# Ordering the instructions of a two-layer RWKV-7 / Hyena / mixture-of-experts kernel with the simulator's timeline model

## Chip, cores and metric

The kernel runs on one core of one Trainium2 chip. The metric is the device time of one execution in microseconds (us), lower is better. TensorE is called PE here, its weight loads PEld, VectorE is DVE, ScalarE is ACT, GpSimd is POOL, and SyncE, which issues most DMAs, is SP.

## What is computed

Two layers over 512 latent and 256 context tokens of width 1024, in fp32. The reference, cut to what matters:

```python
for l in range(2):
    p = modulate(x, shift, scale) @ w_in[l]          # 43 blocks of 128 columns, context tokens too
    y_r = rwkv7(p_rwkv)                              # two scans over the tokens, forward and backward:
    #   S <- S diag(w) + (S (-kk)) (kk*a)^T + v k^T ; y = S r        8 heads x 64
    y_h = x0 * (irfft(rfft(v*x1) * rfft(filt)) + bias * (v*x1))      # long convolution, 512 channels
    g_r, g_h = split(sigmoid(p_gate))
    s = (g_r * (y_r @ w_branch[0]) + g_h * (y_h @ w_branch[1])) @ w_out
    x = layer_norm(alpha * x + gate * s)
    # mixture of experts: best of 4 groups by its two best scores, then two experts inside it
    x = layer_norm(alpha * x + gate2 * moe(modulate(x)))
```

In the second layer the context tokens are no longer carried past the start of the scans, so its row counts are smaller (512 tokens in the gates, where the first layer has 512 and 256).

## The kernel before

The body is Python that emits instructions in program order inside a `tile.TileContext`. The order in which an engine gets its instructions is not the order of the Python text: the context's scheduler takes the instructions that are ready, by the priority they were emitted with and by a table of durations for each kind of instruction, and writes out one fixed list for each engine. Each engine then works its list strictly from the top, and waits where an operand is not there. Two stretches are scheduled apart, because a loop whose number of rounds is only known on the chip (experts with more rows than their place; no round runs here) lies between them: everything up to that loop in the first layer, and all after it.

Each layer goes through these stages:

- **project** (L733 to L1088): the modulated input times `w_in`, each block of 128 columns split into a high and a low part (`hi`, `lo`, L588, L589) and multiplied in three passes (matmuls `pl` for latent and `px` for context tokens, L853 to L860), and the Hyena convolution by matrices of the discrete Fourier transform. For each channel group and segment the convolution is a chain: transposes `hz<-con,zf` (L1005), split in hi and lo, the forward transform (matmuls of `mm3`, L593 to L595, `dft...` tables), products on DVE and POOL (L1015 to L1020), transposes `hz<-con,Y` (L1026), split again, and the inverse transform (`idft...` tables). Blocks of the projection can stand between these links.
- **RWKV** (L1108 on, class `Rwkv`): per pair of token chunks a front part (small matmuls `psl` L248, `pE` L310, `pO` L311, with DVE, ACT and POOL work between), the inverse of a triangular matrix (chain of `pw` L417, `pz` L425, `pw` L435, `pz` L445 with DVE at both ends), then the chain over chunks (L494 to L532). There are three such pairs in each layer. Into this stage the second part of the gates is emitted last (L1126 to L1136): for each of 6 (first layer) or 10 (second layer) blocks of 128 gate columns eight matmuls `gp` (L1133) over 512 tokens, and in the first layer eight more over 256, one sigmoid (L1135) and a store. `gp` has one PSUM bank. `GATES = (10, 6)` (L38) is the number of gate blocks that are computed earlier.
- **branch and merge** (L1220 to L1360): `pb` (the two branches times `w_branch`, with L593 to L595), `po` (the product with `w_out`), the residual and LayerNorm on DVE (L1315 to L1342), the result `h` stored by SP to `hd` (L1344), transposed (`ph`, L1350) and taken through the router matmul (`plg`, L1354), then the routing on DVE (L1554 to L1600).
- **experts** (L1602 on): SP loads the expert weights in 1 MB pieces (`raw<-in_w_exp`, L2148), reads expert numbers into registers (L1887, and L1837 for the number of rounds), POOL gathers token rows (`xg<-hd,idx`, L1924), and PE multiplies (`acc`, L2000 and L2003).

```python
for j in range(GATES[l], 16):                        # L1126
    ...
    for a, n in segs:                                # 512 tokens, and 256 in the first layer
        p = gp.tile([128, 512], F32, name="gp", tag="gp")
        for k in range(8):
            nc.tensor.matmul(p[:, :n], raw[k // 4][:, k % 4], self.gx[...], start=k == 0, stop=k == 7)   # L1133
```

## Time and profile before

| what | us |
|---|---|
| three runs | 3240.1, 3251.25, 3238.47 (median 3240.1) |
| the profiled execution | 3255.05, of which the span is 3253.3 |
| busy in the span | PE 2942.1, DVE 1668.5, ACT 1127.5, POOL 573.6 |
| first layer | project 0 to 526, RWKV 526 to 892, branch and merge to 1117, experts to 1784 |
| second layer | project to 2151, RWKV to 2530, branch and merge to 2660, experts to 3254 |

The busy time of an engine is the time in which at least one of its instructions ran; the stages were cut by hand at the instructions that open them. The profiled execution is one run, and differs from the median of the others by 15 us. The fp32 matmuls without a split appear as two records each in the trace, so that `x6` of `L1133` stands for three matmuls.

### The profile page before, as it was taken

To read this page: it belongs to the slowest core of one execution; us is meant where nothing else is said; L and a number is where in the kernel's file an instruction comes from. 1 tells how busy PE (TensorE), PEld (TensorE's weight loads), DVE (VectorE), ACT (ScalarE), POOL (GpSimd) and SP (SyncE) were. 2 spreads that over 40 slices of the span, in tenths; PEclk is the share of its full clock that TensorE was granted. 3 is DMA by queue.
4 is the path that set the end of the run, shared out by engine and by line. 5 is a ranking of instruction groups with operands and counts; after the bars stand their busy time and mean duration, and the time that the engine had idled before them with its cause. 6 is when DMAs were issued, how large, how long until landed. Compare 5 with 4: busy or idle time off the path is not lost. (4 is left out here: it accounts for less than half of the span.)

```text
span 3253.3 us, 61441 instructions
## 1 busy us (share of the span) xinstructions
PE 2942.1 (90%) x25238; PEld 2018.5 (62%) x25238; DVE 1668.5 (51%) x2981; ACT 1127.5 (35%) x2293; POOL 573.6 (18%) x458
## 2 busy tenths in 40 slices
PE   7999999888888799999997999979889879999994
PEld 5877866676677566555663767646666655444551
DVE  4466534787766544435645347447876571111223
ACT  3453225566421233323422434255554221111111
POOL 1001221354004200000022001254340120000002
PEclk8999999899999799999998899987999979999997
DMA  5453274111244689998895464451112549999995
GB/s 225 126 154 99 80 254 137 51 50 52 84 149 166 242 337 367 358 351 328 322 359 216 153 198 121 156 174 57 50 50 87 205 168 360 383 402 421 383 373 235
DMA packets 220870, 689.83 MB, mean 212 GB/s; under 512 B 71813, under 2 KB 99750, under 8 KB 169128
## 3 DMA queue, kind: packets, MB, share of 16 engines
q1 hardware_dynamic: 186280, 588.62, 49.0%
q10 hardware_dynamic: 26448, 70.73, 6.1%
q0 software_dynamic: 7856, 26.49, 2.3%
q8 instruction: 202, 3.31, 0.4%
q14 instruction: 84, 0.69, 0.1%
HBM read 621.46 MB, written 64.30 MB: 211 GB/s over the span
## 5 line engine op out<-in xcount | busy, mean ns | idle before, releaser
L2000 PE MATMUL acc<-raw,x 128*64 128x256 f32 (+1 forms) x7168 | 569.8, 334 | 13.7 <-DMA raw<-in_w_exp 13.6
L2000 PEld LDWEIGHTS acc<-raw,x 128*64 128x64 f32 (+1 forms) x7168 | 358.3, 125 | 213.9 <-issue 90.9
L589 DVE TENSOR_TENSOR lo<-raw,hi 128x1024 fp32r<-128x1024 f32 x190 | 229.5, 1231 | 303.2 <-ACT hi L588 295.9
L2003 PE MATMUL acc<-raw,a 128*64 128x512 f32 (+2 forms) x1376 | 292.6, 602 | 7.3 <-DMA raw<-in_w_exp 6.2
L588 ACT CAST hi<-raw 128x1024 fp32r<-128x1024 f32 x190 | 193.5, 1048 | 294.6 <-PE px L857 149.9
L2031 DVE TENSOR_TENSOR act<-acc,act 128x256 f32<-128x256 f32 (+1 forms) x98 | 42.1, 430 | 442.5 <-PE acc L2000 400.2
L853 PE MATMUL pl<-xh,hi 128*128 128x512 f32 x560 | 228.1, 407 | 0.2
L858 PE MATMUL pl<-xh,lo 128*128 128x512 f32 x560 | 224.7, 401 | 0.3 <-DVE lo L589 0.3
L854 PE MATMUL pl<-xl,hi 128*128 128x512 f32 x560 | 224.1, 400 | 0.0
L2003 PEld LDWEIGHTS acc<-raw,a 128*64 128x64 f32 (+2 forms) x1376 | 79.0, 130 | 179.9 <-issue 160.5
L1133 PE MATMUL gp<-gx,raw 128*128 128x512 f32 (+1 forms) x352 | 174.2, 612 | 1.6 <-ACT gs L1135 1.5
L1924 POOL DMA_INDIRECT xg<-hd,idx x31 | 31.5, 1015 | 780.8 <-PE pt L1942 706.1
L853 PEld LDWEIGHTS pl<-xh,hi 128*128 128x128 f32 x560 | 107.0, 191 | 44.3 <-issue 20.3
L2026 ACT ACTIVATE act<-acc 128x256 f32<-128x256 f32 (+1 forms) x98 | 38.0, 387 | 241.3 <-PE acc L2000 206.0
L2051 ACT COPY a<-pt 128x256 f32<-128x256 f32 (+2 forms) x86 | 28.5, 349 | 261.6 <-PE pt L2046 261.6
L858 PEld LDWEIGHTS pl<-xh,lo 128*128 128x128 f32 x560 | 107.2, 191 | 18.3 <-issue 10.1
L2057 DVE TENSOR_TENSOR sum<-acc,sum 64x512 f32<-64x512 f32 x82 | 56.4, 687 | 117.6 <-ACT sum L2056 116.9
L854 PEld LDWEIGHTS pl<-xl,hi 128*128 128x128 f32 x560 | 107.1, 191 | 13.7 <-issue 6.2
L311 PE MATMUL pO<-T,K 128*128 128x192 f32 (+1 forms) x320 | 84.9, 378 | 29.0 <-DVE T L330 27.4
L856 PE MATMUL px<-xh,hi 128*128 128x256 f32 x376 | 110.2, 294 | 0.0
L2056 ACT COPY sum<-acc 64x512 f32<-64x512 f32 x82 | 47.6, 580 | 179.3 <-PE acc L2003 178.2
L857 PE MATMUL px<-xl,hi 128*128 128x256 f32 x376 | 108.5, 289 | 0.1
(607 smaller groups left out, 6178.0 us busy)
## 6 DMA issues: line engine op xcount, KB each, us to landing
raw<-in_w_exp SPq DMA_DIRECT2D x384, 1024.0 KB
mraw<-in_w_mod SPq DMA_DIRECT2D x64, 512.0 KB
raw<-in_w_in SPq DMA_DIRECT2D x36, 512.0 KB
rkk<-rkk SPq DMA_DIRECT2D x24, 768.0 KB
raw<-in_w_in ACTq DMA_DIRECT2D x34, 512.0 KB
mraw<-in_w_mod SPq DMA_DIRECT2D x12, 1024.0 KB
raw<-in_w_in SPq DMA_DIRECT2D x32, 256.0 KB
wb<-in_w_branch SPq DMA_DIRECT2D x32, 256.0 KB
```

Source lines behind the costliest of these rows:

```text
L311: nc.tensor.matmul(pO[:, jj, 0:192], lO, T[c][kO, j, 1, :], start=True, stop=True)
L588: self.nc.scalar.copy(hi, src)
L589: (engine or self.nc.vector).tensor_tensor(lo, src, f32(hi), ALU.subtract)
L853: mm(pl, hi[:, k], xh[:, k, L], start=f, stop=False)
L854: mm(pl, hi[:, k], xl[:, k, L], start=False, stop=False)
L856: mm(px, hi[:, k], xh[:, k, X], start=f, stop=False)
L857: mm(px, hi[:, k], xl[:, k, X], start=False, stop=False)
L858: mm(pl, lo[:, k], xh[:, k, L], start=False, stop=e)
L1133: nc.tensor.matmul(p[:, :n], raw[k // 4][:, k % 4], self.gx[:, k, a - T0:a - T0 + n], start=k == 0, stop=k == 7)
L2000: mm(a[w * g:w * g + w, 0:4 * w], x, raw[:, 4 * w * g:4 * w * g + 4 * w], start=k == 0, stop=k == 7)
L2003: mm(a[w * g:w * g + w], x, raw, start=k < G, stop=k >= 8 - G)
L2057: tt(t, a[o:o + 64], t, ALU.add)
```

## The change

The context is told to schedule with the simulator's timeline model: while it picks the next instruction for each engine it takes ready times and durations from that model, and no longer from its own table. Priorities, tiles, buffers, semaphores and the program itself stay as they are.

```diff
-    with tile.TileContext(nc) as tc:
+    with tile.TileContext(nc, schedule_with_timeline_sim=True) as tc:
         Kern(tc, A).run()
```

The number and kind of the instructions on each engine are the same, but for four fewer ACT_TABLE_LOADs on ACT, which follow from the order of its functions. What moves is the order; three places are shown.

**PE at the entry of RWKV in the second layer.** `hz` L710 is the modulation, `gp` the gates, `psl`, `pE` and `pO` the front part, `pw` L417 the first step of the first inverse. Before:

```order
L710 MATMUL hz<-mraw,c_78 32x512 x7
L1133 MATMUL gp<-gx,raw 128x512
L724 MATMUL pq<-mrow,con 2x512
L1133 MATMUL gp<-gx,raw 128x512
L248 MATMUL psl<-lw,w_16284 128x128 x4
L1133 MATMUL gp<-gx,raw 128x512 x2
L248 MATMUL psl<-la,a_16285 128x128 x4
L1133 MATMUL gp<-gx,raw 128x512 x2
L248 MATMUL psl<-lw,w_16284 128x128 x4
```

With the change:

```order
L1133 MATMUL gp<-gx,raw 128x512 x8
L710 MATMUL hz<-mraw,c_78 32x512 x6
L1133 MATMUL gp<-gx,raw 128x512 x8
L724 MATMUL pq<-mrow,con 2x512
L1133 MATMUL gp<-gx,raw 128x512 x8
L248 MATMUL psl<-lw,w_16284 128x128 x4
L1133 MATMUL gp<-gx,raw 128x512 x8
L248 MATMUL psl<-la,a_16285 128x128 x4
L1133 MATMUL gp<-gx,raw 128x512 x8
L248 MATMUL psl<-lw,w_16284 128x128 x4
```

Whole groups of eight now stand between the pieces of the front part. In the second layer 24 of the 80 `gp` matmuls stood ahead of the first `pw` of L417, now all 80. In the first layer 16 of 48 with 512 columns and 15 of 48 with 256 stood ahead of it, now 48 and 40.

**PE in the Hyena convolution of the first layer**, one link of its chain: the transposes `hz<-con,Y` and what follows them. `pl` and `px` are blocks of the projection. Before:

```order
L1026 MATMUL hz<-con,Y 128x128 x3
L858 MATMUL pl<-xh,lo 128x512
L1026 MATMUL hz<-con,Y 128x128 x3
L860 MATMUL px<-xh,lo 128x256
L853 MATMUL pl<-xh,hi 128x512
L854 MATMUL pl<-xl,hi 128x512
L856 MATMUL px<-xh,hi 128x256
L593 MATMUL hz<-idftlh,yh 128x256
```

With the change, the like link of the last channel group:

```order
L593 MATMUL hz<-dftlh,zh 128x384
L594 MATMUL hz<-dftll,zh 128x384
L595 MATMUL hz<-dftlh,zl 128x384
L1026 MATMUL hz<-con,Y 128x128 x6
L593 MATMUL hz<-idftlh,yh 128x256
L594 MATMUL hz<-idftll,yh 128x256
L595 MATMUL hz<-idftlh,yl 128x256
```

No block stands between the links there; in the last two channel groups of the first layer nine links follow one another like this, and runs of 16 and 21 rows of blocks stand between others.

**PE and SP in the merge of the second layer.** On PE before, where `po` is the output product of later tokens and `ph`, `plg` the transposes and router product of `h`:

```order
L593 MATMUL po<-oh,mh 128x512
L1350 MATMUL ph<-con,h__23749 128x128 x4
L594 MATMUL po<-ol,mh 128x512
L595 MATMUL po<-oh,ml 128x512
L593 MATMUL po<-oh,mh 128x512
L594 MATMUL po<-ol,mh 128x512
L1350 MATMUL ph<-con,h__23749 128x128 x4
L1354 MATMUL plg<-wrt,hT 128x16 x4
```

On PE with the change, from the last `po` on:

```order
L595 MATMUL po<-oh,ml 128x512
L1350 MATMUL ph<-con,h__23680 128x128 x8
L1354 MATMUL plg<-wrt,hT 128x16 x8
L1350 MATMUL ph<-con,h__23749 128x128 x8
L1354 MATMUL plg<-wrt,hT 128x16 x8
L1350 MATMUL ph<-con,h__23864 128x128 x8
```

On SP before, where `hd` is the store of `h`, `raw` a weight load, and L1887 reads an expert's number:

```order
L1344 DMA hd<-h__23680 128x1024
L1344 DMA hd<-h__23749 128x1024
L2148 DMA raw<-in_w_exp 128x2048
L1344 DMA hd<-h__23864 128x1024
L2148 DMA raw<-in_w_exp 128x2048 x2
L1344 DMA hd<-h__23933 128x1024
L2148 DMA raw<-in_w_exp 128x2048 x9
L1887 TENSOR_LOAD eid
```

On SP with the change:

```order
L1344 DMA hd<-h__23680 128x1024
L1344 DMA hd<-h__23749 128x1024
L2148 DMA raw<-in_w_exp 128x2048 x10
L1344 DMA hd<-h__23864 128x1024
L1344 DMA hd<-h__23933 128x1024
L1887 TENSOR_LOAD eid
```

All `po` now stand ahead of the first `ph`; ten weight loads, where there were three, stand ahead of the last `hd` store; and SP reads 12 expert numbers at once, where it read three and went on with weights.

## Rows read from the trace of the kernel before

**Rows 1.** The page: span, busy time of PE, and its clock in 40 slices.

```profile
span 3253.3 us, 61441 instructions
...
PE 2942.1 (90%) x25238; PEld 2018.5 (62%) x25238; DVE 1668.5 (51%) x2981; ACT 1127.5 (35%) x2293; POOL 573.6 (18%) x458
...
PEclk8999999899999799999998899987999979999997
```

**Rows 2.** Busy time in stretches; `(x...)` counts records; last clock, DMA share, GB/s.

```profile
core 0: us, PE busy (x) PEld busy (x) DVE busy (x) ACT busy (x) POOL busy (x), PEclk, DMA share, GB/s
...
100.00:526.00 426.00, 408.05 (x2243) 318.38 (x2241) 204.78 (x321) 145.25 (x229) 58.77 (x66) 0.98 0.47 148
526.00:601.50 75.50, 61.17 (x308) 41.18 (x304) 60.30 (x117) 51.69 (x142) 32.14 (x34) 0.86 0.26 85
601.50:864.00 262.50, 237.69 (x4207) 185.75 (x4207) 201.63 (x417) 144.09 (x409) 94.43 (x78) 0.93 0.18 57
...
2151.00:2217.00 66.00, 54.96 (x265) 33.70 (x264) 47.83 (x93) 47.76 (x136) 35.35 (x41) 0.84 0.33 107
...
2660.00:3254.00 594.00, 528.00 (x4555) 270.41 (x4554) 130.54 (x264) 85.07 (x184) 43.51 (x31) 0.95 0.90 358
```

**Rows 3.** Timeline of PE in RWKV of the first layer: start, duration, instruction.

```profile
534.03 2.84 PE L1133 MATMUL gp<-gx,raw 128*128 128x512 f32 x6
...
547.89 3.72 PE L1133 MATMUL gp<-gx,raw 128*128 128x256 f32 x16
...
554.51 1.98 PE L1133 MATMUL gp<-gx,raw 128*128 128x512 f32 x4 [0.54 <-ACT gs L1135]
```

**Rows 4.** Busy time of the gates alone (L1133), PE and PEld, by stretch.

```profile
601.50:864.00 262.50, 56.88 (x131) 23.39 (x130) 0.93 0.18 57
...
2217.00:2530.00 313.00, 62.42 (x112) 20.05 (x112) 0.90 0.21 65
```

**Rows 5.** Busy time inside RWKV: fronts, and inverses with gates in them.

```profile
680.00:710.00 30.00, 22.55 (x132) 16.74 (x132) 27.74 (x49) 16.86 (x52) 13.32 (x12) 0.77 0.18 58
710.00:741.00 31.00, 30.23 (x612) 22.78 (x612) 25.65 (x59) 16.75 (x42) 7.65 (x6) 1.00 0.14 40
790.00:816.00 26.00, 19.04 (x102) 12.50 (x103) 25.20 (x43) 11.60 (x34) 11.86 (x10) 0.80 0.05 16
...
2217.00:2252.00 35.00, 32.77 (x640) 22.89 (x640) 22.47 (x56) 15.40 (x39) 7.07 (x7) 0.81 0.13 40
```

**Rows 6.** Chain of waits, 2217 to 2327: pieces of the path.

```profile
2217.24 3.42 PE pw L417 x128
...
2227.15 3.38 PE gp L1133 x4
```

**Rows 7.** Chain of waits, 2327 to 2424: a piece of the path.

```profile
2327.35 2.04 PE pw L417 x126
```

**Rows 8.** Timeline of PE in the first layer's Hyena convolution.

```profile
359.37 0.60 PE L1005 MATMUL hz<-con,zf 128*128 128x128 f32 x4
...
361.93 0.44 PE L593 MATMUL hz<-dftlh,zh 128*128 128x384 f32 x1
...
366.62 0.33 PE L595 MATMUL hz<-dftlh,zl 128*128 128x384 f32 x1
...
368.75 0.55 PE L1026 MATMUL hz<-con,Y 128*128 128x128 f32 x3 [0.50 <-POOL Y L1019]
```

**Rows 9.** Busy time at the end of the first layer's chain.

```profile
864.00:892.00 28.00, 22.97 (x320) 18.20 (x319) 24.80 (x56) 19.60 (x42) 0.00 (x0) 0.94 0.22 73
```

**Rows 10.** Timeline of DVE in the second layer's merge.

```profile
2632.10 0.17 DVE L1355 COPY lgt<-plg 128x16 f32<-128x16 f32 x1 [4.16 <-PE plg L1354]
...
2642.12 0.17 DVE L1355 COPY lgt<-plg 128x16 f32<-128x16 f32 x1 [1.38 <-PE plg L1354]
...
2653.69 0.17 DVE L1355 COPY lgt<-plg 128x16 f32<-128x16 f32 x1 [5.36 <-PE plg L1354]
```

**Rows 11.** Timeline of all engines, from the second layer's merge to its experts.

```profile
2638.38 0.33 SPq L2148 DMA_DIRECT2D raw<-in_w_exp  x1
...
2664.59 1.22 POOL L1924 DMA_INDIRECT xg<-hd,idx  x1 [9.34 <-DVE x L1712]
...
2673.30 1.54 PE L1942 MATMUL pt<-con,xg 96*128 96x96 f32 x8 [9.78 <-DMA xg<-hd,idx]
```

**Rows 12.** What SP's queue waited for: total us, times, longest.

```profile
SPq L2148 <- PE acc L2000: 459.9, 183, 27.1
```

**Rows 13.** SP at L1887, the reading of expert numbers: ns min/median/max, first and last start.

```profile
L1887 SPq TENSOR_LOAD <-eid x30: 260/270/469, 1110.8 to 3122.1; - x30
L1887 SPq FUSED_REGOPS  x30: 147/152/181, 1111.3 to 3122.4; - x30
```

**Rows 14.** Groups of instructions: a table load on ACT, busy time and mean ns.

```profile
L1135 ACT ACT_TABLE_LOAD x13 | 16.7, 1283 | 0.2
```

## The prediction

> **What bounds the kernel now.** I read the page first. PE is busy in 2942.1 of 3253.3 us, 90%, and no other engine comes near it [rows 1]; so a new order can gain at most what PE is idle or runs at a low clock, and it can lose wherever it puts PE work where something was waiting behind PE. The clock row shows which stages run below full speed [rows 1]. Then I read the stretches one by one, because the 90% is a mean over stages with different limits [rows 2]. In the first project stage PE is busy for 408.05 of 426 us. In the last expert stage the DMA share is 0.90. The stretches in which PE isn't the only limit are the entries of RWKV (61.17 of 75.5 us, clock 0.86, and 54.96 of 66 us, clock 0.84) and the fronts and inverses after them. There the path goes from PE to DVE and back. Third, I read those pieces closely [rows 5]: in the thin fronts DVE is busy for 27.74 of 30 and 25.20 of 26 us, and PE for 22.55 and 19.04.
>
> My sum is made against the profiled execution, 3255 us. That run is 15 us above the median 3240 of the runs shown, so I take 15 off at the end. Half a per cent of the median, 16 us, is about what a measurement of this kernel can tell from no change.
>
> **The change, part 1: gates ahead of the first inverse.** In the second layer 56 more `gp` matmuls of 512 columns stand ahead of the first `pw`; in the first layer 32 more of 512 columns and 25 of 256. Three of 512 take 2.84 us, 0.947 each, and eight of 256 take 3.72 us, 0.465 each [rows 3]. So the first layer gets 32 x 0.947 + 25 x 0.465 = 41.9 us of PE work ahead of its first inverse, and the second 56 x 0.947 = 53.0 us. PE runs its list from the top, and the pieces of the front part stand between the groups of eight, so the front's last piece comes later by what PE cannot do in time in which it idled. That time is 75.5 - 61.17 = 14.3 us in the first layer and 66 - 54.96 = 11.0 us in the second [rows 2]. DVE, ACT and POOL work of the front lies beside these gates; it isn't longer than before.
>
> What remains depends on the clock. In the stretches where gates fill PE the granted clock was 1.00, the upper level of 2.4 GHz (710 to 741, PE busy for 30.23 of 31 us); in thin ones it was 0.77 and 0.80, a mixture of 2.4 and 1.2 GHz [rows 5]. With whole groups of gates the entry is a full stretch, so I price the gates at full clock, a tenth cheaper than the row, which is what the two levels allow at a mean clock of 0.90: 38 and 48 us. First layer: 38 - 14.3 = +24. Second: 48 - 11 = +37. Bounds: nothing absorbed, +42 and +53; or all absorbed and the old work speeded up to 1.00 too, which saves 61.17 x 0.14 = 8.6 and 54.96 x 0.16 = 8.8 more, +15 and +28. I stay between them, since the old work there is small matmuls that wait for other engines, and one PSUM bank for `gp` makes a next group wait for the sigmoid of the last (0.54 us before the gates at 554.51 [rows 3]).
>
> The Trainium skill, page "TensorE: Matmul & The Clock Gate", section "HAM oscillation — how this bites in real kernels", says that gaps in PE's work put the array back to its lower clock, and that work in full stretches keeps it high. By this the entry would come out at its low bound, 18 us under my sum in all. The thin and full stretches above agree with it in direction.
>
> **Part 2: what the loop behind the first inverse gives back.** Those gates leave the three inverses and fronts, where they took 56.88 us in the first layer and 62.42 in the second [rows 4]. If PE were the only limit there, all 41.9 and 53.0 us would come back. Two views speak against that. In the thin fronts DVE was busy nearly throughout [rows 5]; gates there stood beside it. And the chain of waits of the second layer between 2217 and 2327 holds 8.3% of `gp`, 9.1 us, nearly all in pieces like the one at 2227.15 [rows 6], and between 2327 and 2424 it holds 3.7%, 3.6 us, both summed over the lines of that view. So the path saves about 13 us in the second layer, and by the ratio of the moved work about 10 in the first. Bounds: 0, if a dependent step merely waits longer for DVE, and the whole 42 and 53. I take 13 and 10, as the path was read directly.
>
> RWKV together: 24 - 10 + 37 - 13 = **+38**.
>
> **Part 3: project.** In the last two channel groups of the first layer's convolution nine links of the chain follow each other with no block of the projection between. A link takes about 1.9 us from one set of matmuls to the next: 359.97 (end of `zf` transposes) to 361.93, and 366.95 to 368.75 [rows 8]. PE waits for 9 x 1.9 = 17 us where blocks covered that before. Some of the 18 us that PE idled between 100 and 526 [rows 2] goes away, since runs of 16 and 21 rows of blocks stand at other links; I take 6 off, and add 1 for two modulation loads that stand behind input weights on SP. **+12**, between 0 (all made good elsewhere) and +25. The second layer's project has the same pattern with fewer links: **+3**, 0 to +8.
>
> **Part 4: chain tail.** The first branch's `pb` matmuls now stand between the last steps of the chain. PE idled for 5 of 28 us at the first layer's tail [rows 9]; filling half of it is -3, and -5 in the second layer, whose chain has more such steps. Bounds 0 and -16, -20, if all of `pb` of that branch went under the chain.
>
> **Part 5: merge.** Before, DVE waited 4.16, 1.38 and 5.36 us for `plg` results while it had LayerNorm work of later tokens behind them [rows 10]. With all `po` ahead of `ph` these waits end for LayerNorm, and the last `plg` comes earlier: -8 in the second layer of the 10.9 us, -5 in the first, **-13**. Bounds 0 and -24.
>
> **Part 6: the rest.** SP reads all expert numbers at once. A read takes SP 0.27 + 0.15 us [rows 13], 15 of them 6.3 us, and PE nothing, as SP then waits for a weight buffer anyhow; those waits sum to 459.9 us [rows 12]. Without that cover the 6.3 us would be added in each layer. The last expert stage is bound by its weights (DMA share 0.90 [rows 2]): 0, between -5 and +5. Four table loads fewer at 1.283 us [rows 14] are 5 us of ACT, most of it off the path: **-2**.
>
> Sum: 38 + 12 + 3 - 8 - 13 - 2 = +30, so 3285 for a profiled run and **3270 us** against the median.
>
> **Rivals.**
>
> A. *PE bounds the loop after all; faster.* PE is busy for 237.69 of 262.5 us behind the first inverse [rows 2], 91%, which speaks for it; the rows of DVE speak against it. If all gates give back their time, RWKV comes to 24 - 42 + 37 - 53 = -34, and with +15 - 8 - 13 - 2 the sum is -42: 3213 profiled, **3198 us**. It decides from the point where the loop gives back more than 61 us, the two entries' cost.
>
> B. *The clock falls where the fillers were; slower still.* The same first step of an inverse took 3.42 us for 128 records at 2217 [rows 6] and 2.04 for 126 at 2327 [rows 7], with clock 0.81 in the first stretch [rows 5]. An inverse has two such steps (`pw`, `pz`) and two of a third their size, so about 3.5 us more at the lower level. If the eight inverse halves that ran at 1.00 fall to it, that is +28; nothing more is given back elsewhere. 3270 + 28, **about 3300 us**. For it speaks that PE loses 57 of 238 us of work in that loop.
>
> C. *The last `hd` stores come too late.* The gather in the second layer is issued at 2664.59, and PE waits 9.78 us for it [rows 11]. Ten loads of 1.05 MB now stand ahead of the last two stores; at the 358 GB/s of that stage [rows 2] they need 29 us. The first load was let go at 2638.38, when a `po` matmul freed its buffer [rows 11], so the stores would land at about 2668 and the gather would begin some 4 us later instead of 8 earlier: **about 3285 us**. It decides if the loads are not let go 8 us earlier, as I assume from the shorter `po`. The Trainium skill, page "DMA: Bandwidth & Descriptors", section "Queues, rings and completion order", says that each DMA engine takes the descriptors of a ring in order, which would let the stores wait for the weights; no row here shows a store behind ten loads.
>
> D. *The parts cancel; no change.* The loop gives back about 60 us instead of 23, short of rival A: **about 3234 us**.
>
> That the change does nothing is no rival: the order differs in every stage.
>
> **How the numbers follow.** The forecast gets 0.45 and by itself lies between 3250 and 3295. A gets 0.20, B 0.15, C 0.08, D 0.12. Slower by over 0.5% (above 3256): nearly all of the forecast, B and C, 0.45 + 0.15 + 0.08 less 0.08 for its lower edge, 0.60. Faster by over 0.5% (below 3224): A and a little of D, 0.22. Within: 0.18. The range 3205 to 3315 leaves out the lower half of A and the upper part of B.
>
> **What would show it.** Right: the first `pw` of L417 starts about 35 us later in the first layer (that includes project's +12) and the second layer's entry stretch grows by about 37; the loops behind it shorten by 5 to 20 us; gates have nearly no records there; the clock in the entry is 0.95 or more. Links of the last Hyena groups show PE idle of about 2 us each. The waits for `plg` on DVE are gone. Wrong: the loop behind the first inverse shortens by 30 us or more in each layer (A), `pw` at 3.4 us in most inverses (B), or a gather that starts after `hd` landed later than the routing (C).

## The result, and the profile after

The changed kernel takes 3356.9 us (median of 4 runs, 3352.2 to 3370.6), the kernel before 3245.2 (median of 4): 1.0359 times as long, 95% interval 1.0332 to 1.0385. The way was forecast, the size was not: 3270 was predicted, and 3357 lies beyond the upper end of the range, 3315. The two profiled executions have spans of 3253.3 [rows 1] and 3350.4 us, 97 us apart; the argument below is about those 97.

The page of the changed kernel: span, busy time, and PE's clock in 40 slices.

```profile
span 3350.4 us, 61522 instructions
...
PE 2984.6 (89%) x25238; PEld 2082.7 (62%) x25238; DVE 1668.3 (50%) x2981; ACT 1122.9 (34%) x2289; POOL 578.0 (17%) x458
...
PEclk9999999986888789999999799897787879999997
```

PE has the same 25238 matmul records and is busy 42 us longer, 37 of them in the RWKV stages (entries and loops), whose loops run at a lower clock; the rest of the 97 us is PE idle.

The time by stage, from the timelines of PE. Project ends with the last projection block (L853 to L858), entry with the first `pw` (L417), loop with the last `pz` (L445), tail with the first `po`, merge with the first `acc` of the experts (L2000), and the first layer's experts with the last `acc` of that line. So the first layer's last products (L2003, until 1758.4 us before and 1824.7 with the change) count to the second project stage, and 7 of the 20.2 us that it got shorter are theirs. The forecast's -2 for the rest is not in the table.

| stage | before | after | difference | forecast |
|---|---|---|---|---|
| layer 1: project | 524.1 | 556.6 | +32.5 | +12 |
| entry of RWKV | 77.4 | 100.9 | +23.5 | +24 |
| loop of RWKV | 263.5 | 286.0 | +22.5 | -10 |
| tail | 110.3 | 109.9 | -0.4 | -3 |
| merge | 141.7 | 143.6 | +1.9 | -5 |
| experts | 604.8 | 598.4 | -6.4 | 0 |
| layer 2: project | 424.5 | 404.3 | -20.2 | +3 |
| entry of RWKV | 71.0 | 115.2 | +44.3 | +37 |
| loop of RWKV | 267.2 | 265.1 | -2.1 | -13 |
| tail | 94.8 | 99.1 | +4.3 | -5 |
| merge | 95.7 | 92.4 | -3.3 | -8 |
| experts | 578.4 | 578.9 | +0.5 | 0 |

The same stretches in the kernel before and in the changed kernel; the columns are those of [rows 2]. Before:

```profile
524.10:601.50 77.40, 63.08 (x322) 41.60 (x320) 61.39 (x121) 53.46 (x145) 33.66 (x39) 0.87 0.26 84
601.50:865.00 263.50, 237.99 (x4213) 185.99 (x4212) 201.63 (x417) 144.09 (x409) 94.43 (x78) 0.93 0.18 57
2146.30:2217.20 70.90, 59.66 (x284) 34.68 (x283) 49.78 (x98) 51.49 (x142) 39.89 (x52) 0.85 0.35 114
2217.20:2484.40 267.20, 240.60 (x4143) 181.46 (x4143) 197.86 (x407) 139.00 (x398) 93.38 (x79) 0.89 0.18 57
```

After:

```profile
0.00:556.60 556.60, 504.03 (x2636) 383.93 (x2636) 248.86 (x393) 182.45 (x286) 63.56 (x73) 0.96 0.46 149
556.60:657.50 100.90, 94.75 (x426) 58.10 (x425) 62.24 (x122) 61.79 (x153) 39.54 (x45) 0.95 0.29 93
657.50:943.50 286.00, 221.54 (x4155) 195.87 (x4154) 200.78 (x420) 135.71 (x403) 88.06 (x72) 0.80 0.14 44
...
2199.70:2314.90 115.20, 104.98 (x404) 51.02 (x404) 48.47 (x96) 63.89 (x149) 58.25 (x61) 0.94 0.42 136
2314.90:2580.00 265.10, 216.86 (x4092) 193.04 (x4092) 195.50 (x414) 132.60 (x400) 90.86 (x75) 0.76 0.14 42
```

The entries are full of gates, at a clock of 0.95 and 0.94. The loops have lost nearly all of them: in the first layer PE is busy for 221.54 us where it was for 237.99, and the loop is 22.5 us longer all the same, at a clock of 0.80 where it was 0.93. A chain step of PE, L512, shows two things that changed. Before:

```profile
L512 PE MATMUL pB<-SB,U 128*128 128x128 f32 x160 | 22.3, 283 | 0.3 <-ACT SB L509 0.2
```

After:

```profile
L512 PE MATMUL pB<-SB,U 128*128 128x128 f32 x160 | 28.3, 332 | 15.3 <-ACT SB L509 15.3
```

The mean of one goes from 283 to 332 ns (at the lower clock), and the idle time ahead of it from 0.3 to 15.3 us: it now waits for ACT's copy `SB`. DVE too waits longer, for ACT and for PE. Its waits in the loop before, and then after:

```profile
DVE R L522 <- PE pB L512: 13.6, 8, 3.4
...
DVE T L331 <- ACT T L326: 7.9, 10, 2.7
DVE U L329 <- ACT T L324: 4.6, 7, 1.3
```

```profile
DVE U L329 <- ACT T L324: 24.9, 13, 8.4
DVE R L522 <- PE pB L512: 24.8, 9, 6.4
...
DVE T L331 <- ACT T L326: 4.9, 6, 2.0
```

ACT was busy for 135.71 of 286 us in that loop, so its load alone does not explain these waits; which of them goes with the length of the loop is read further down, from the runs with the engines' orders put back.

### The profile page after: what moved, and what is told of

It is laid out like the page before. It is cut to its first block, busy times and chain, and to the rows that moved or that the text cites. A ratio compares the mean times of both kernels' runs of the same rounds, so it can differ in the third digit from the quotient of the medians.

```text
span 3350.4 us, 61522 instructions
## 1 busy us (share of the span) xinstructions
PE 2984.6 (89%) x25238; PEld 2082.7 (62%) x25238; DVE 1668.3 (50%) x2981; ACT 1122.9 (34%) x2289; POOL 578.0 (17%) x458
## 5 line engine op out<-in xcount | busy, mean ns | idle before, releaser
L2000 PE MATMUL acc<-raw,x 128*64 128x256 f32 (+1 forms) x7168 | 574.2, 334 | 2.3 <-DMA raw<-in_w_exp 1.6
L2000 PEld LDWEIGHTS acc<-raw,x 128*64 128x64 f32 (+1 forms) x7168 | 360.6, 125 | 203.1 <-issue 88.1
L2003 PE MATMUL acc<-raw,a 128*64 128x512 f32 (+2 forms) x1376 | 295.1, 603 | 11.9 <-DMA raw<-in_w_exp 11.0
L2031 DVE TENSOR_TENSOR act<-acc,act 128x256 f32<-128x256 f32 (+2 forms) x98 | 42.0, 429 | 410.6 <-PE acc L2000 368.4
L853 PE MATMUL pl<-xh,hi 128*128 128x512 f32 x560 | 228.9, 409 | 7.5 <-ACT t L1073 4.8
L858 PE MATMUL pl<-xh,lo 128*128 128x512 f32 x560 | 225.7, 403 | 0.0
L2003 PEld LDWEIGHTS acc<-raw,a 128*64 128x64 f32 (+2 forms) x1376 | 78.0, 129 | 181.2 <-issue 152.9
L1133 PE MATMUL gp<-gx,raw 128*128 128x512 f32 (+1 forms) x352 | 148.6, 573 | 11.1 <-ACT gs L1135 11.1
L853 PEld LDWEIGHTS pl<-xh,hi 128*128 128x128 f32 x560 | 107.7, 192 | 42.6 <-issue 8.3
L858 PEld LDWEIGHTS pl<-xh,lo 128*128 128x128 f32 x560 | 108.0, 193 | 21.7 <-issue 10.7
L1133 PEld LDWEIGHTS gp<-gx,raw 128*128 128x128 f32 x352 | 68.2, 201 | 77.9 <-issue 59.6
L860 PE MATMUL px<-xh,lo 128*128 128x256 f32 x376 | 109.7, 292 | 0.0
```

The source lines that it names most:

```text
L853: mm(pl, hi[:, k], xh[:, k, L], start=f, stop=False)
L858: mm(pl, lo[:, k], xh[:, k, L], start=False, stop=e)
L860: mm(px, lo[:, k], xh[:, k, X], start=False, stop=e)
L1133: nc.tensor.matmul(p[:, :n], raw[k // 4][:, k % 4], self.gx[:, k, a - T0:a - T0 + n], start=k == 0, stop=k == 7)
L2000: mm(a[w * g:w * g + w, 0:4 * w], x, raw[:, 4 * w * g:4 * w * g + 4 * w], start=k == 0, stop=k == 7)
L2003: mm(a[w * g:w * g + w], x, raw, start=k < G, stop=k >= 8 - G)
```

## Experiments

The theories at the start. **G**: the gates' new place on PE costs, at the entry by their own time and in the loop by the lower clock. **S**: the other reorderings cost. The stage lengths of all runs stand in one table behind the last of them; PE's clock is told where it matters.

**Gates held in the loop, and gates alone moved.** The first run keeps the timeline model and ties the gates to the matmul groups of the inverses (`marks`, four for each inverse); the second keeps the old scheduler and ties the first `pw` behind the last gate. (`ISSUE_ORDER` stands for an edge that only sets the order of two instructions on one engine; "..." marks what is left out.)

```diff
...
+                    if done >= free:
+                        m = rw.marks[(done - free) * len(rw.marks) // (many - free)]
+                        tc.add_manual_dep(i.ins, m.name, ISSUE_ORDER, reason="hold")
+                    done += 1
```

```diff
+        for j in range(GATES[l], 16): ...          # the gates, emitted here
         rw.run()
-        for j in range(GATES[l], 16): ...
...
+                    if len(self.marks) == 1 and e + hc + h == 0:
+                        self.tc.add_manual_dep(i.ins, self.last.ins.name, ISSUE_ORDER, reason="ahead")
```

> The changed kernel, but each gate matmul beyond the first 32 (first layer) or 24 (second layer) is tied, by an issue-order edge on PE, behind one of the 24 matmul groups of the inverses, so that the gates lie spread through RWKV as before the change. Theory G (gates taken out of the loop cost the time, at the entry directly and in the loop by the lower clock): entry from the last projection block to the first pw back from 102.7 and 115.7 us to about 78 and 72; loop from the first pw to the last pz 264 and 267 us (after: 286 and 265) at clock 0.90 or more; the whole near 3270 us. Rival S (the other reorderings inside the fronts and inverses lengthen the loop): entry falls by about 65 us in all, but the loop stays at 286 or takes the gates on top (320); the whole 3300 to 3350 us.

> The kernel before with its own scheduler, and one thing changed: all gate matmuls are issued ahead of the first inverse of their layer. Theory G: entry 78 to about 103 us and 71 to about 116 us; the loop without gates at clock 0.75 to 0.85 and no shorter than before (263 to 290 us, 260 to 270 us); the whole slower by 65 to 95 us, near 3320. Rival P (PE bounds the loop): the loop shrinks by 40 us in each layer and the whole stays within 20 us of 3245. Rival S: the whole slower by 45 us or less, since the loop loses the 23 us of the forecast.

Measured: 3370.8 us for the held gates, ratio 1.037 (1.033 to 1.042), and 3339.1 for the gates ahead, 1.027 (1.024 to 1.031). Holding them helped nothing: loops 287 and 293 us, entries 93 and 106. Moving them in the old scheduler cost 90 us. Three of its stretches, the first loop, the second entry and the second loop:

```profile
618.30:914.50 296.20, 237.83 (x4240) 206.45 (x4240) 220.17 (x443) 148.49 (x444) 108.67 (x89) 0.76 0.14 45
2199.10:2292.70 93.60, 90.72 (x311) 43.23 (x310) 39.10 (x84) 46.44 (x110) 28.82 (x43) 0.98 0.37 122
2292.70:2580.80 288.10, 233.34 (x4173) 204.31 (x4172) 209.19 (x425) 143.76 (x434) 107.45 (x88) 0.74 0.14 42
```

The loops without gates are 33 and 21 us longer than with them, so rival P (PE bounds the loop) fell. But in this run the scheduler planned every other engine anew around the moved gates, so its 90 us are not the gates' alone, and the two runs pull against each other: moving the gates cost 90 us, and giving their place back brought nothing.

**One engine's order put back at a time.** The helper ties instructions of one engine in the order that the kernel before had (names are equal in both), and leaves the rest free. Called at the end of RWKV's emission, with a table for each engine:

```diff
+def pin_order(tc, tables):
+    seen = {i.name: i for i in tc.nc.cur_bb.bb.instructions}
+    for runs in tables:
+        order = [seen[n] for k, c in runs for j in range(c) if (n := f"I-{k + j}") in seen]
+        for a, b in zip(order, order[1:]):
+            ...
+            tc.add_manual_dep(b, a.name, ISSUE_ORDER, reason="pinned")
...
-        s_inv.close()
+        s_inv.close(); pin_order(tc, PIN[l])
```

In the first of these two PIN holds PE in RWKV; in the second also PE in the first layer's project.

> The changed kernel with one thing put back: issue-order edges give PE, within RWKV of both layers up to the last gate, the order of the kernel before, gates included; DVE, ACT, POOL and SP and all other stages stay as the timeline model orders them. Theory G (the order on PE, gates above all, is what costs in RWKV): entries 77 and 71 us and loops 264 and 267 us within 10 us each, clock 0.9; the whole 3357 - 88 = about 3270 us. Rival S (the order of DVE, ACT, POOL and SP in RWKV costs, as the run with gates held in the loop let one think, whose loops stayed at 287 and 293 us): loops stay at 285 or more, the whole 3330 or more.

> As the run before it, and PE's order in the first layer's project stage is put back too. If bare links of the convolution on PE are the cause of that stage's 32 us, it falls from 557 to 530 us or less, and the whole to about 3240, since the second layer's project keeps its 20 us; if the order of loads or of the other engines is the cause, the stage stays at 545 or more and the whole at 3265 or more.

Measured: 3368.6 us, 1.039 (1.036 to 1.042), and 3353.5, 1.034 (1.031 to 1.037). With PE's old order, gates included, RWKV is as long as with the new (774.5 us in all four stretches of the first of these runs, 767.2 in the changed kernel). The first layer's loop in that run:

```profile
649.80:943.20 293.40, 254.07 (x4259) 202.31 (x4258) 199.76 (x416) 141.64 (x408) 88.58 (x72) 0.87 0.16 51
```

Theory G fell as the whole story. The project stage came to 552 us where the run beside it has 559, so PE's order there, bare links of the convolution included, gives back 7 us by itself.

**The gates alone, with PE's order fixed, and fillers in their place.** The old scheduler, PE's RWKV order fixed as it was, but the 65 and 56 gates behind the first `pw` moved into the entry and spread evenly over it (PIN has them there); and the same with as many unread matmuls, all of 512 columns, where they had been.

```diff
+        p = gp.tile([128, 512], F32, name="fill", tag="gp")
+        fill = [nc.tensor.matmul(p, self.gx[:, i % 8, 0:128], self.gx[:, i % 8, 0:512], start=True, stop=True).ins for i in range(FILL[l])]
+        pin_order(tc, PIN[l], fill, l * OFF)
```

> The kernel before, its PE order in RWKV pinned as it was, but with the 65 and 56 gate matmuls that followed the first pw moved evenly into the entry. Theory C (without the gates between them the inverses and chain steps run at the lower clock): loops 285 to 300 and 280 to 295 us at clock 0.75 to 0.80; entries 90 to 100 us; the whole 3320 to 3350. Rival P (PE bounds the loop): loops shorter than 240 us.

> The same as the run before it, and at each place that a gate matmul left, a matmul of 512 columns whose result nobody reads: 121 matmuls, about 104 us of PE work, that are no part of the computation. Theory C: the loops come back to 264 to 275 us at clock 0.88 or more, so the whole is 20 to 45 us shorter than without that work, about 3300. Rival D (the loop's length comes from the order of dependent steps, not from the clock): the loops stay or grow, and the whole is as long as without it or up to 104 us longer.

Measured: 3416.0 us, 1.054 (1.051 to 1.058), and 3408.7, 1.051 (1.046 to 1.055). Entries are 70 us longer in the first of them, more than the moved gates' price (46 and 53 us, at the 0.947 and 0.465 us that the prediction read for one). Spread one by one, all gates together kept PE busy for 87.47 and 91.92 us there, where the changed kernel's whole groups took 64.34 (8 gates of 256 columns fewer) and 79.03:

```profile
523.20:670.10 146.90, 87.47 (x192) 34.13 (x192) 0.90 0.20 66
2216.70:2357.30 140.60, 91.92 (x160) 27.76 (x160) 0.92 0.28 89
```

`gp`, which has one PSUM bank, also waited 17.9 us for `gs` in the first layer's entry. The loops without and with fillers:

```profile
670.10:941.30 271.20, 220.54 (x4129) 191.01 (x4128) 201.88 (x413) 134.35 (x398) 86.89 (x72) 0.78 0.14 45
...
2357.30:2645.50 288.20, 229.12 (x4085) 198.28 (x4084) 198.64 (x407) 132.47 (x392) 87.66 (x73) 0.73 0.13 39
```

```profile
682.70:954.60 271.90, 248.70 (x4213) 185.17 (x4214) 202.68 (x412) 132.22 (x394) 87.69 (x72) 0.94 0.14 44
...
2370.60:2644.50 273.90, 247.70 (x4144) 185.44 (x4143) 197.04 (x403) 129.21 (x386) 87.61 (x73) 0.87 0.13 40
```

Taking the gates out gives nothing back: 271 and 288 us where 264 and 267 stood with them. The fillers alone, in these two loops:

```profile
682.70:954.60 271.90, 69.53 (x130) 22.89 (x130) 0.94 0.14 44
2370.60:2644.50 273.90, 60.96 (x101) 18.66 (x101) 0.87 0.13 40
```

They are 130 us of PE's time, not the 104 that the expectation had. They raise the clock from 0.78 to 0.94 and from 0.73 to 0.87 and lengthen neither loop; the second gets 14 us shorter, the first stays, so neither C nor D holds in both. The 0 and 14 us are what the higher clock gives less what the fillers take; no run separates the two, so the clock's own share stays open. The first entry, with the same order on PE in both runs, took 162 us with fillers behind it and 147 without; that difference is not explained.

**All engines, or all but PE.** PIN holds PE, DVE, ACT, POOL and SP in RWKV, and then all of them but PE. (The `xd` rows that the texts call context rows are the latent rows of the residual, reloaded and scaled at L1056 to L1059.)

> The changed kernel with the order of all engines (PE, DVE, ACT, POOL, SP) within RWKV of both layers put back to that of the kernel before, with the reload of the context rows (xd) ahead of it in the second layer; everything else stays with the timeline model. Theory S2 (with PE's order alone put back RWKV stayed 95 us too long, so it is the order of DVE, ACT, POOL and SP there that costs): entries back to 77 and 71 us and loops to 264 and 267, each within 8 us, the whole near 3357 - 88 = 3270. Rival N (what comes into RWKV from the stages ahead, loads and buffers that come free late, costs): RWKV stays 40 us or more too long, the whole 3305 or more.

> As the run before it, but PE is left to the timeline model in RWKV; DVE, ACT, POOL and SP, with the stores and loads of the gates, have the order of the kernel before. Theory S2: the loops are 271 to 290 us long as in the run whose gates alone were moved, entries up to 20 us longer than before; the whole 3280 to 3310. Rival G (the place of the gates on PE alone costs the 88 us): the whole within 15 us of 3357. As the gates' sigmoids and stores are held late, PE may put the gates back by itself; then this run equals the one before it.

Measured: 3317.6 us, 1.021 (1.019 to 1.023), and 3431.3, 1.056 (1.054 to 1.058). The first layer's loop with all engines, and then with all but PE (whose gates went back into the loop there too):

```profile
637.40:905.50 268.10, 241.18 (x4259) 190.07 (x4258) 202.48 (x417) 144.78 (x410) 94.86 (x78) 0.92 0.18 56
```

```profile
651.20:950.40 299.20, 246.17 (x4258) 201.13 (x4256) 200.49 (x417) 145.33 (x414) 94.74 (x78) 0.86 0.16 50
```

This settles the first layer's loop. With every engine in its old order it is back within 5 us of the kernel before, and so is the second layer's, which the change had not lengthened. With one half of the engines old and the other new it is 293 and 282, or 299 and 319, longer than with either order whole. The loop's length isn't made by one engine's list but by how the lists fit.

DVE's waits in the first layer's loop say where it shows. With PE's order alone put back, and then with all engines':

```profile
DVE T L331 <- ACT T L326: 22.3, 13, 5.0
DVE U L329 <- ACT T L324: 19.6, 12, 4.2
DVE R L522 <- PE pB L512: 11.8, 6, 3.2
```

```profile
DVE R L522 <- PE pB L512: 13.6, 8, 3.4
...
DVE T L331 <- ACT T L326: 9.0, 9, 2.6
...
DVE U L329 <- ACT T L324: 5.6, 6, 1.3
```

The three sum to 26.1 us before and 54.6 with the change, to 53.7 with PE's order alone put back, 57.3 with all but PE's, and 28.2 with all; the loops took 264, 286, 293, 299 and 268 us. With the gates alone moved the sum is 36.9 and with fillers 35.3, in loops of 271 and 272. The idle time ahead of L512 doesn't go with the loop. With PE's order alone put back, and then with fillers, it is

```profile
L512 PE MATMUL pB<-SB,U 128*128 128x128 f32 x160 | 22.6, 284 | 3.4 <-ACT SB L509 3.3
```

```profile
L512 PE MATMUL pB<-SB,U 128*128 128x128 f32 x160 | 22.3, 282 | 0.3 <-ACT SB L509 0.3
```

in loops of 293 and 272 us. So PE's wait for `SB` is time that gates or fillers cover, and not what makes this loop long.

One thing stayed: the second layer's entry took 106 us with 24 gates in it.

**Project stages.** All engines put back in the first layer's project and in RWKV of both; and, in the kernel before, the second layer's project alone ordered as the timeline model orders it.

> The changed kernel with all engines' order put back in the first layer's project stage and in RWKV of both layers; the second layer's project, the merges, and the experts stay with the timeline model. If stage costs add: 3357 - 32 - 88 = 3237, with the 20 us that the second layer's project gained and the 3 to 6 us of merge and experts that is a little faster than before (3220 to 3240). If the gain of the second layer's project was only borrowed from RWKV behind it (work and loads put off), 3250 to 3265.

> The kernel before, with its own scheduler, and only the second layer's project stage ordered on all engines as the timeline model orders it. If its 20 us are real: 3245 - 20 = 3225, and faster than both. If they are borrowed from the entry of RWKV behind it (the reload of context rows and the modulation put off): the stage 20 us shorter, the entry 20 us or more longer, the whole 3240 to 3265.

Measured: 3284.8 us, 1.011 (1.009 to 1.012), and 3249.7, 1.001 (0.999 to 1.003). The first layer's project is back to 530 us. The second layer's is 27 us shorter in the kernel before as well, and the entry behind it 25 us longer: borrowed.

**The late reload.** ACT's first fills of RWKV (`T`, L213) read nothing of the reload of the residual rows, yet a run below has one wait 27.0 us for it; the reading is that they need the memory that it holds. POOL's last operation of it (first and last start of four) before, and after:

```profile
L1058 POOL TENSOR_TENSOR t<-t,lnb x4: 2337/2424/3232, 2101.7 to 2144.0; 128x1024 f32<-128x1024 f32 x4
```

```profile
L1058 POOL TENSOR_TENSOR t<-t,lnb x4: 2337/2364/2680, 2180.6 to 2241.3; 128x1024 f32<-128x1024 f32 x4
```

It ended with the last projection block before (2146.4 and 2146.3) and 44 us behind it now (2243.7 and 2199.7). I tried to make it shorter, in both kernels:

```diff
             for tb in range(2, 6):
-                t = rs.tile([128, 1024], F32, name="t", tag="t")
+              for H in (slice(0, 512), slice(512, 1024)):
+                t = rs.tile([128, 512], F32, name="t", tag="t", bufs=2)
...
```

> The changed kernel with the reload of the residual rows at the end of the second layer's project stage (load, two POOL operations, store; the rows that an expectation above called context rows are the latent ones) done in halves through two buffers of 512 columns instead of whole rows through one of 1024, so that a load runs beside the operations of the half before. Theory X (RWKV's first tiles wait for the memory of this reload, which ended 44 us behind the last projection block, where it ended with that block before the change): the reload ends 20 us or more earlier relative to that block, the second layer's entry falls from 115 to 85 to 100 us, the whole to 3330 to 3342. Rival (the 80 gates in the entry are what fills it): the entry stays within 8 us of 115 and the whole within 8 us of 3357.

> The same edit in the kernel before. The reload ended with the last projection block there, so no theory gives it more than a few us: 3235 to 3255, the same. If it comes out 10 us or more faster the reload was on the path before too.

Measured: 3349.0 us, 1.033 (1.030 to 1.035), and 3249.8, 1.002 (1.000 to 1.003). The reload still ended 39 us late, because its parts were again queued behind fills of RWKV on POOL, and the entry fell by 7 us only. This edit didn't move what it was to move and tells little. Then I left the reload out, with all engines of RWKV in their old order:

```diff
-            for tb in range(2, 6):
+            for tb in range(0):
```

> The run with all engines' order in RWKV put back, and the reload of the residual rows at the end of the second layer's project stage left out (it is part of the computation). With the gates back in the loop, the second layer's entry still took 106 us there, and ACT's fill of RWKV's first tiles waited 27 us for the reload's last POOL operation. Theory X (two causes lie side by side in that entry, 80 gates and the late reload, and each alone holds it near 100 us): the entry falls from 106 to 72 to 85 us, the whole from 3318 to 3285 to 3300. Rival M (the modulation and loads that the timeline model puts behind the last projection block fill it): the entry stays at 95 or more.

Measured: 3282.1 us, 1.011 (1.007 to 1.015). The entry falls from 106 to 76.9 us. So the late reload alone holds that entry near 105 us; 80 gates alone hold it at 93.6 (the run with gates ahead, whose reload ended with the last projection block, at 2199.2 and 2199.1). In the run with all engines in their old order ACT's wait reads

```profile
ACT T L213 <- POOL t L1058: 27.0, 1, 27.0
```

**SP in the first layer's project.** PIN holds PE in that project and in RWKV, and SP in that project.

> As the run with PE's order put back in the first layer's project stage and in RWKV, with SP's order of transfers in that project stage put back as well. Theory L (the loads come in another order and PE waits for them): the project stage falls from 552 to 535 us or less, near the 530 that it had with all engines put back. Rival E (the order on ACT and DVE, in front of the projection blocks, holds it): 545 us or more.

Measured: 3340.2 us, 1.029 (1.026 to 1.032). The project stage is 525 us, 27 less than with PE's order alone, so what held it there is the order of SP's transfers. (SP's old order with PE's new one was not run.) The stage without and with SP's old order:

```profile
0.00:552.20 552.20, 492.95 (x2636) 376.76 (x2636) 246.44 (x393) 184.55 (x286) 64.38 (x73) 0.94 0.46 150
```

```profile
0.00:525.20 525.20, 484.76 (x2636) 370.04 (x2636) 244.06 (x393) 182.76 (x285) 64.33 (x73) 0.97 0.48 158
```

**A version that might beat both.** The kernel before with PE and SP of the second layer's project in the new order, and the reload tied ahead of RWKV's fills; and the changed kernel with that tie alone. The edit is again a PIN table: on POOL each of RWKV's first memsets stands behind the last L1058, on ACT each L213 behind the last L1059.

```diff
-        s_inv.close()
+        s_inv.close(); pin_order(tc, PIN[l])
```

> The kernel before with its own scheduler; in the second layer's project stage PE and SP have the timeline model's order, and the reload of the residual rows is tied ahead of RWKV's first fills on POOL and ACT, as it stood before the change. If what the timeline order gains in that stage is real once the reload isn't late: stage and entry together 475 to 485 us (495 before, 494 with the late reload), the whole 3228 to 3238, a little faster than before. If it is borrowed: together 490 or more, the whole 3242 to 3255.

> The changed kernel, and only that reload tied ahead of RWKV's first fills on POOL and ACT. If gates and reload are two causes side by side in the second layer's entry, the 80 gates alone keep it near 94 to 108 us and the whole at 3335 to 3352; if the reload is the larger and the gates only fill its wait, the entry falls to 90 or less and the whole to 3330 or less.

Measured: 3259.3 us, 1.005 (1.003 to 1.007), and 3365.3, 1.038 (1.035 to 1.041). Stage and entry together take 491.9 us where they took 495.5, so the gain of the second layer's project is borrowed, nearly all of it. In the changed kernel the tie left the reload where it was (its last L1057 starts at 2240.5), as its loads came no earlier, and the entry at 116. How gates and reload share that entry in the changed kernel itself stays open. No version beat the kernel before.

Stage lengths in us, from the profiled executions (P project, E entry, L loop, with the layer's number):

| run | P1 | E1 | L1 | P2 | E2 | L2 |
|---|---|---|---|---|---|---|
| before | 524 | 77 | 264 | 424 | 71 | 267 |
| after | 557 | 101 | 286 | 404 | 115 | 265 |
| gates held in the loop | 557 | 93 | 287 | 398 | 106 | 293 |
| old scheduler, gates ahead | 524 | 94 | 296 | 416 | 94 | 288 |
| PE old in RWKV | 559 | 91 | 293 | 407 | 108 | 282 |
| and in project 1 | 552 | 90 | 292 | 401 | 104 | 286 |
| gates alone moved | 523 | 147 | 271 | 416 | 141 | 288 |
| with fillers | 521 | 162 | 272 | 418 | 143 | 274 |
| all engines old in RWKV | 557 | 81 | 268 | 396 | 106 | 271 |
| all but PE old in RWKV | 556 | 95 | 299 | 406 | 107 | 319 |
| all old in project 1, RWKV | 530 | 79 | 266 | 400 | 104 | 272 |
| before, project 2 new | 525 | 78 | 261 | 398 | 96 | 266 |
| after, reload in halves | 557 | 101 | 283 | 406 | 108 | 270 |
| before, reload in halves | 522 | 79 | 265 | 426 | 69 | 267 |
| all old in RWKV, no reload | 558 | 79 | 266 | 405 | 77 | 268 |
| PE old, SP old in project 1 | 525 | 89 | 300 | 407 | 105 | 284 |
| before, PE and SP of project 2 new | 526 | 79 | 260 | 404 | 88 | 270 |
| after, reload tied ahead | 557 | 101 | 283 | 401 | 116 | 267 |

## Why the prediction was wrong, step by step

- **Which stage**: right that RWKV decides and that the sign is slower. RWKV costs 88 of the 97 us, of which the second project stage gives back 20; 38 were forecast.
- **Part 1, the entries**: +24 and +37 forecast, +23.5 and +44.3 measured. The price of the gates on PE was right: L1133 keeps PE busy for 38.1 and 50.4 us more in the entries, and 38 and 48 were priced. Before, and then after:

```profile
524.10:601.50 77.40, 26.23 (x62) 12.33 (x62) 0.87 0.26 84
2146.30:2217.20 70.90, 28.62 (x48) 9.18 (x48) 0.85 0.35 114
```

```profile
556.60:657.50 100.90, 64.34 (x174) 33.38 (x174) 0.95 0.29 93
2199.70:2314.90 115.20, 79.03 (x160) 31.64 (x160) 0.94 0.42 136
```

  The idle time that they were to use up was not: 14.3 and 11 us were counted, but PE's idle time fell by 8.2 us in the first entry and by 1.0 in the second. The old work there got 6.4 and 5.1 us shorter, which the sum had only in its low bounds; that the first entry came out at +24 is in part luck. And the gates are not the only cause. With PE's order alone put back the entries are 91 and 108 us, with all engines put back 81 and 106. In the second a reason holds that the sum didn't have: the reload of the residual rows, 44 us late, keeps the entry at 105 us even with the gates away. Gates and reload lie side by side there, and the prediction read PE's list for this place and not POOL's and ACT's. By the page that it cited ("TensorE: Matmul & The Clock Gate" of the Trainium skill, section "HAM oscillation — how this bites in real kernels") the entries should have come to their low bounds, +15 and +28; the clock did as the page says, 0.95 and 0.94, the time did not.
- **Part 2, what the loop gives back**: the step that failed. It said that the path saves 10 and 13 us. It read how much of the chain of waits is `gp`, and took that the chain without it is the old one, shortened. With the gates alone moved the loops were 7.7 and 21 us longer, and with everything moved +22.5 and -2.1. That was 43 us of the 67 that the sum missed. What it left out is the order on the other engines: put back on PE alone it changed nothing (loops 293 and 282), put back on all it brought 18 of the first loop's 22.5 us, and DVE's waits fell with it from 54.6 to 28.2. In the second layer the new order as a whole costs the loop nothing (265 us, and 271 with all put back).
- **Part 3, project**: +12 and +3 forecast, +32.5 and -20.2 measured; the two errors nearly cancel. Bare links were priced at 17 us, and the changed kernel has them: in the first layer's convolution PE idles for 24.4 us where it idled for 6.8. Before, and then after:

```profile
300.00:416.00 116.00, 109.21 (x665) 94.55 (x664) 67.41 (x127) 31.26 (x55) 28.37 (x22) 1.00 0.23 78
```

```profile
331.00:457.00 126.00, 101.58 (x555) 88.71 (x554) 57.77 (x104) 26.42 (x48) 24.71 (x21) 0.89 0.20 67
```

  The term that was too small is SP's order, priced at 1: PE's order put back took 7 us off the stage, SP's on top of it 27 more. In the second layer the 20 us are the entry's loss.
- **Parts 4 and 5, tail and merge**: -21 forecast, +2.5 measured, the other 24 of the 67 us. The `pb` matmuls do lie between the chain's steps now, and the time comes back behind it. PE in the first layer's tail:

```profile
1014.02 0.79 PE L593 MATMUL pb<-y0h,hi 128*128 128x512 f32 x1 [11.93 <-ACT hi L588]
```

and ACT just before:

```profile
1010.19 1.04 ACT L588 CAST oh<-wo 128x1024 fp32r<-128x1024 f32 x1 [3.92 <-DMA wo<-in_w_out]
1012.40 1.04 ACT L588 CAST oh<-wo 128x1024 fp32r<-128x1024 f32 x1 [1.17 <-DMA wo<-in_w_out]
1013.35 0.61 ACT L588 CAST hi<-wb 128x512 fp32r<-128x512 f32 x1
```

  The leftover `pb` of the first branch had covered most of the norm of the second (PE waited 4.44 us there before); now nothing does, and the cast that PE waits for is queued on ACT behind two casts that wait for their weights. The forecast named what is filled and not what loses its cover. This is read from the trace; no run took it apart.
- **Part 6**: the experts 6.4 us shorter, just outside its bounds of 5, and 0.5 longer.
- **Rivals**: A fell, as no loop gave its gates' time back. B had the direction (the clock fell from 0.93 to 0.80 and from 0.89 to 0.76) and the time nearest, 3300, but not the mechanism alone: with fillers, at 0.94 and 0.87, the loops were 0 and 14 us shorter net of the fillers' own time, where it priced 28 for the kernel. C did not come up: PE waited 5.3 us for the gather where it waited 9.78 [rows 11]. D fell.

## What to carry to other kernels

A new order for in-order engines is not the sum of the moves on the busiest one: compare the lists of every engine at each place where two of them hand work back and forth, and take a stage whose hand-overs are dense as at risk by more than the matmuls that moved (here 22.5 us in one loop and none in the other). Work that filled the gaps of a path bound by hand-overs gave nothing back here when it left (loops 7.7 and 21 us longer without it), and was paid for where it went (+23.5 and +44.3 us in the changed kernel). A stage that got shorter is a gain only if the one behind it didn't get longer; the two are read as a sum.

## What was not expected of the hardware

Some 130 us of unread matmuls made a kernel no slower (3408.7 against 3416.0 us): the clock rose from 0.78 to 0.94 in one loop, which stayed as long as it was, and from 0.73 to 0.87 in the other, which got 14 us shorter. By PE's busy times in the first loop, 41 of the 69.5 us that the fillers took came out of the other matmuls (220.5 us without fillers, 179.2 with them), and 27 out of idle time (50.7 us without, 23.2 with).

Where a matmul stands changed what it cost: 80 gates in the second layer's entry kept PE busy for 79.03 us in whole groups of eight, at a clock of 0.94, and for 91.92 us spread one by one between the small matmuls of the front, at 0.92.
